# Packed constants, host-laid weights, joined u and v, and a planner with 24 rank settings in a one-layer encoder kernel

## The chip, the cores and the metric

The kernel runs on one core of a Trainium2 chip. The metric is the device time of one launch in microseconds (us). PE is TensorE with PEld its weight loads, DVE is VectorE, ACT is ScalarE, POOL is GpSimd, SP is SyncE, which issues most transfers.

## The reference

One layer of a bidirectional encoder on 1024 tokens of 1024 channels, all in float32:

```
h  = RMSNorm(x);  z = h @ w_in                      # 1024 x 3072, split into cv cg | lx lg | su sv
A  = silu(groupnorm(dwconv31(cv * sigmoid(cg))))    # 256 channels
B  = (rglru_fwd(lx) + rglru_bwd(lx)) * gelu(lg)     # 512 channels, gates from 8 heads of 64x64
C  = gelu(su) * (W_s layernorm(gelu(sv)) + b)       # 256 channels, chunks of 128 tokens
x  = x + concat(RMSNorm(A), RMSNorm(B), RMSNorm(C)) @ w_out
x  = x + (gelu(fg) * fu) @ w_down                   # fg, fu = halves of dwconv3(RMSNorm(x) @ w_up), 2 x 2816
x  = x + sigmoid(RMSNorm(x) @ w_ple_gate + b) * RMSNorm(p @ w_ple)
out = RMSNorm(x)
```

## The kernel before

Every float32 product is made of three matmuls of a rounded type (`mm3`): each operand is split into a high and a low part (`split`: ACT rounds the high part, DVE subtracts it), and high x high, high x low and low x high are summed in PSUM. A moving operand has 512 columns where it can.

The program is recorded first and ordered afterwards. Engine proxies (`Eng`, `Order.rec`) collect operations with costs; `rank` gives each a due time, counted back from the PE work in the order of recording, with three weights (`STRETCH`, how much slower than its cost a non-PE operation is taken to be; `FETCH`, how far ahead of its use a load is due; `DRAIN`, when a PSUM tile is to be emptied); `schedule` is a greedy list scheduler over the five queues (some ACT and DVE operations may change engine); `replay` runs the order through a model of waits and transfers, and its landing times go into the next of six rounds. The order with the shortest replay is issued. In the trace every instruction therefore has one line, L461, and is told apart by its tiles.

The stages, in the order of recording:

- Head. The eight tiles of x are loaded with SP (`load_x`, fixed first), normed, transposed by PE into hT, and multiplied into the first half of lx, two column tiles in matmuls of 256 columns.
- Constants. Fourteen small parameters are loaded by fifteen loads on POOL's queue (`rows`), as rows of 128 values, into tile V; `const_T` turns them into columns with five PE transposes, copies them out of PSUM with DVE (to cA, cB, cO in sm, cF) and makes what is derived from them: halves, sums, negatives, and log-sigmoid of lambda by a polynomial on 128x8 values.
- LRU (`lru(i)`, four blocks, two directions each): four taps over 1024 tokens, the first on ACT or DVE with scale and bias from cA, three on DVE; split; 12 matmuls against the gate weights; tanh, exp, sqrt; a scan on DVE. The gate weights of a block (`lru_gate_w`) are a memset of POOL and four POOL loads of 64x64 blocks into a 128x512 tile, then a split into V.
- Convolution (`conv_a`): 31 taps as 47 DVE operations of 512 columns per channel tile, from the gated product of cv and cg.
- p: its two halves are loaded token-major, transposed by PE (16 transposes), split, multiplied by w_ple and stored to DRAM (e).
- C: su and sv are two products with tokens on partitions (`token_major`), 256 columns each, sv first within each half of the tokens; `W0` to `W3` hold sv's weights, `W4`, `W5`, `G2`, `G3` those of su. The four spatial weight matrices are loaded as they are and transposed by PE. Then lg's products reuse W0 to W3.
- Join. C is scaled by a statistic that needs A's, transposed (`pt<-ident,xA`), and the first pass of w_out starts (`w_out_pass`).
- Up projection with a seven-product scheme on 256-column weight blocks (`prep_up`, `up_pair`, 20 of them, and two plain ones), the width-3 convolution and the gate on ACT and DVE; g goes through DRAM. Down projection, gate and final norm follow.

Weight blocks of 256 columns come through `load_cols`, in pieces of 256 values (1 KB):

```
S.dma_start(out=r[q], in_=w[q * 512:(q + 1) * 512, c0:c0 + 256].rearrange("(k p) c -> p k c", p=P))
```

Of the kernel before, what the change touches and what calls it, by code (L numbers as in the profile page):

```python
# [10 lines left out]
F32 = mybir.dt.float32  # L11
# [12 lines left out]
STRETCH = 2.2  # L24
DRAIN = 1.0
FETCH = 14.0
# [5 lines left out]
RATE = 330e3  # L32
ROUNDS = 6
# [25 lines left out]
class Vw:  # L59
# [18 lines left out]
    def flat(self):  # L78
        return Vw(self.tl, self.chain + [("rearrange", ("p a b -> p (a b)",))], self.idx.reshape(1, -1))
# [30 lines left out]
class Order:  # L110
# [125 lines left out]
    def rank(self):  # L236
# [6 lines left out]
        for op in self.ops:  # L243
            if op.eng != "P":
                for tl, m, w in op.acc:
                    if tl.psum and not w:
                        op.prio = min(op.prio, DRAIN + max(o.prio for o, _ in tl.wr if o.num < op.num))
        for op in reversed(self.ops):
            for d in op.deps:
                c = FETCH if d.calls[0][0] == "dma_start" else d.cost * (1 if d.eng == "P" else STRETCH)  # L250
                d.prio = min(d.prio, op.prio - c)
# [10 lines left out]
    def plan(self):  # L262
# [66 lines left out]
    def share(self, jobs):  # L329
        jobs.sort(key=lambda j: j[0])  # L330
        act, fin, t, i = {}, {}, 0.0, 0
        while i < len(jobs) or act:
            k = min(act, key=act.get) if act else None
            done = t + act[k] * len(act) / RATE if act else float("inf")
            step = min(done, jobs[i][0] if i < len(jobs) else float("inf"))
            for q in act:
                act[q] -= (step - t) * RATE / len(act)
            t = step
            if step == done:
                del act[k]  # L340
                fin[k] = t
            else:
                act[jobs[i][2]] = float(jobs[i][1])
                i += 1
# [128 lines left out]
def encoder_layer(ctx, tc, x, p, norm_mix, w_in, conv_dw_w, conv_dw_b, conv_gn_g, conv_gn_b,  # L473
                  lru_conv_w, lru_conv_b, lru_wa, lru_ba, lru_wx, lru_bx, lru_lambda,
                  sgu_ln_g, sgu_ln_b, sgu_ws, sgu_bs, out_norm, w_out, norm_ffn, w_up,
                  ffn_conv_w, ffn_conv_b, w_down, norm_ple, w_ple_gate, b_ple_gate, w_ple,
                  ple_post_norm, final_norm, out):
# [3 lines left out]
    x, p, out = x[0], p[0, 0], out[0]  # L481
    w_in, w_out, w_up, w_down = w_in[0], w_out[0], w_up[0], w_down[0]
# [57 lines left out]
    eps, cO = sm[:, 95:96], sm[:, 96:112]  # L540
# [7 lines left out]
    cA = blk("cA", [P, 108], F32)  # L548
    cB = blk("cB", [P, 110], F32)
    cS = blk("r16", [P, 32], F32)  # L550
    cF = blk("cF", [P, 176], F32)
    lg4, mv, st6 = cA[:, 76:92].cut(8), cA[:, 92:108].cut(2), cB[:, 62:110].cut(6)
    cB = cB[:, 0:62]

    load_table(AF.Sqrt, eps)

    def rows(dst, r0, n, src):
        G.dma_start(out=dst[r0:r0 + n, :], in_=src)
# [4 lines left out]
    def const_T():  # L563
        ps = pt()
        PE.transpose(ps[:, 0:74], stA[0:74, 0], ident[0:74, 0:74])
        PE.transpose(ps[:, 128:190], stA[0:62, 1], ident[0:62, 0:62])
        PE.transpose(ps[:, 256:272], stO[0:16], ident[0:16, 0:16])
        V.tensor_copy(cA[:, 0:74], ps[:, 0:74])
        V.tensor_scalar(out=cB, in0=ps[:, 128:190], scalar1=0.5, scalar2=None, op0=ALU.mult)
        V.tensor_copy(cO, ps[:, 256:272])  # L570
# [3 lines left out]
        ps = pt()  # L574
        PE.transpose(ps[:, 0:88], stF[0:88, 0], ident[0:88, 0:88])
        PE.transpose(ps[:, 128:216], stF[0:88, 1], ident[0:88, 0:88])
        V.tensor_copy(cF[:, 0:88], ps[:, 0:88])
        V.tensor_copy(cF[:, 88:176], ps[:, 128:216])
# [125 lines left out]
    st = blk("V", [P, 5, P])  # L704
    stA, stF, stO = st[:, 0:2], st[:, 2:4], st[:, 4]
# [10 lines left out]
    rows(stA[:, 0], O_CW, 32, lru_conv_w.rearrange("o d k (t p) -> (o d k t) p", p=P))  # L716
    rows(stA[:, 0], O_CB, 8, lru_conv_b.rearrange("o d (t p) -> (o d t) p", p=P))
    rows(stA[:, 0], O_BA, 8, lru_ba.rearrange("o d (t p) -> (o d t) p", p=P))
    rows(stA[:, 0], O_BX, 8, lru_bx.rearrange("o d (t p) -> (o d t) p", p=P))
    rows(stA[:, 0], O_LAM, 8, lru_lambda.rearrange("o d (t p) -> (o d t) p", p=P))  # L720
    rows(stA[:, 0], O_DB, 2, conv_dw_b.rearrange("o (t p) -> (o t) p", p=P))
    rows(stA[:, 0], O_SB, 4, sgu_bs.rearrange("o h p -> (o h) p"))
    rows(stA[:, 0], O_GN, 2, conv_gn_g.rearrange("o (t p) -> (o t) p", p=P))
    rows(stA[:, 0], O_GN + 2, 2, conv_gn_b.rearrange("o (t p) -> (o t) p", p=P))
    rows(stA[:, 1], 0, 62, conv_dw_w.rearrange("o k (t p) -> (o k t) p", p=P))
    rows(stO, 0, 8, out_norm.rearrange("o (k p) -> (o k) p", p=P))
    rows(stO, 8, 8, norm_ple.rearrange("o (k p) -> (o k) p", p=P))
# [12 lines left out]
    const_T()  # L740
# [133 lines left out]
    for h in range(2):  # L874
        pin = raw([P, 4, 256])
        S.dma_start(out=pin, in_=p.rearrange("(h t p) c -> h p t c", p=P, t=4)[h])
        for q in range(2):
            ps = pt()
# [17 lines left out]
    wsv = prep_cols(w_in, 1792, Mixed("W0", "W1", "W2", "W3"))  # L896
# [4 lines left out]
    S.dma_start(out=wsr, in_=sgu_ws[0].rearrange("h p q -> p h q"))  # L901
# [4 lines left out]
    wsu = prep_cols(w_in, 1536, Mixed("W4", "W5", "G2", "G3"))  # L906
# [488 lines left out]
```

## Time and profile before

| | |
|---|---|
| median of 3 runs | 1138.18 us (1138.13 to 1138.3) |
| profiled execution | 1138.66 us, span 1136.9 us |
| PE busy | 1109.4 us, 5305 matmuls |
| DVE busy | 820.5 us |
| ACT busy | 558.5 us |
| POOL busy | 25.5 us |
| HBM | 97 GB/s over the span |

The span runs from the first to the last instruction of the profiled execution. The ends of matmuls are modelled, so their starts give their pace.

### The profile page before, as it was taken

To read this page: it belongs to the slowest core of one execution; us is meant where nothing else is said; L and a number is where in the kernel's file an instruction comes from. 1 tells how busy PE (TensorE), PEld (TensorE's weight loads), DVE (VectorE), ACT (ScalarE), POOL (GpSimd) and SP (SyncE) were. 2 spreads that over 40 slices of the span, in tenths; PEclk is the share of its full clock that TensorE was granted. 3 is DMA by queue.
4 is the path that set the end of the run, shared out by engine and by line. 5 is a ranking of instruction groups with operands and counts; after the bars stand their busy time and mean duration, and the time that the engine had idled before them with its cause. 6 is when DMAs were issued, how large, how long until landed. Compare 5 with 4: busy or idle time off the path is not lost.

```text
span 1136.9 us, 13205 instructions
## 1 busy us (share of the span) xinstructions
PE 1109.4 (98%) x5305; PEld 929.8 (82%) x5305; DVE 820.5 (72%) x976; ACT 558.5 (49%) x720; POOL 25.5 (2%) x50
## 2 busy tenths in 40 slices
PE   6999999998999999999999999999999999999996
PEld 5987799887888888888888888888788888888885
DVE  6699999977966887687768776949433546654565
ACT  7555864779435475454545454536440222324445
POOL 3100100100000000000000000000000000000000
PEclk9999999999999999999999999999999999999999
DMA  8301240135032122232223222315640426421121
GB/s 296 99 1 56 94 162 20 53 101 185 22 122 96 39 74 93 75 111 74 69 80 112 74 74 75 111 56 192 235 147 2 148 85 212 130 75 40 72 74 55
DMA packets 55629, 110.60 MB, mean 97 GB/s; under 512 B 3977, under 2 KB 36594, under 8 KB 55568
## 3 DMA queue, kind: packets, MB, share of 16 engines
q1 hardware_dynamic: 53280, 104.35, 27.2%
q0 software_dynamic: 2288, 5.41, 1.3%
q8 instruction: 41, 0.67, 0.3%
q14 instruction: 20, 0.16, 0.0%
HBM read 85.63 MB, written 24.12 MB: 97 GB/s over the span
## 4 chain that ended last, share of the span: by engine, by line
PE 82%; DVE 13%; ACT 2%; issue 1%; DMA 1%; SPq 0%; DVEq 0%
PE pm L461 62%; PE pt L461 20%; DVE W L461 6%; DVE L L461 3%; DVE xA L461 1%; DMA xA<-in_x_dram 1%; DVE xB L461 1%; DVE G L461 1%; DVE hT L461 1%; ACT W L461 1%; ACT hT L461 0%; DMA raw<-in_w_down_dram 0%; ACT L L461 0%; ACT L461 0%; DVE V L461 0%
## 5 line engine op out<-in xcount | busy, mean ns | idle before, releaser
L461 PE MATMUL pm<-hT,W 128*128 128x512 f32 (+1 forms) x860 | 194.5, 369 | 0.1
L461 PEld LDWEIGHTS pm<-hT,W 128*128 128x128 f32 x860 | 149.8, 190 | 26.8 <-DVE hT L461 0.4
L461 PE MATMUL pm<-hT 128*128 128x512 f32 x480 | 124.6, 389 | 0.0
L461 PEld LDWEIGHTS pm<-hT 128*128 128x128 f32 x480 | 90.0, 188 | 19.2 <-DVE xA L461 0.4
L461 PE MATMUL pt<-hT,W 128*128 128x512 f32 x336 | 86.1, 389 | 0.0
L461 ACT ACTIVATE W<-raw 128x512 fp32r<-128x512 f32 (+1 forms) x60 | 44.9, 760 | 64.1 <-PE pt L461 47.8
L461 PEld LDWEIGHTS pt<-hT,W 128*128 128x128 f32 x336 | 63.1, 188 | 13.1
L461 DVE TENSOR_TENSOR xB<-xB,pm 128x512 f32<-128x512 f32 (+1 forms) x40 | 37.9, 950 | 42.5 <-PE pm L461 42.2
L461 PE MATMUL pm<-hT,hT 128*128 128x512 f32 (+1 forms) x256 | 66.2, 388 | 0.0
L461 ACT ACT_TABLE_LOAD x47 | 60.3, 1283 | 4.8 <-DVE W L461 2.4
L461 DVE TENSOR_TENSOR W<-raw,W 128x512 fp32r<-128x512 f32 (+1 forms) x57 | 47.1, 835 | 18.6 <-ACT W L461 18.6
L461 PEld LDWEIGHTS pm<-hT,hT 128*128 128x128 f32 x256 | 46.6, 188 | 8.9
L461 PE MATMUL pm<-L,L 128*128 128x512 f32 x160 | 50.3, 389 | 0.0
L461 DVE TENSOR_TENSOR xA<-xA,pm 128x1024 f32<-128x1024 f32 x20 | 24.4, 1219 | 35.1 <-PE pm L461 35.1
L461 DVE TENSOR_TENSOR X<-X,pm 128x512 f32<-128x512 f32 x20 | 13.7, 684 | 49.0 <-PE pm L461 49.0
L461 ACT ACTIVATE L<-raw 128x512 fp32r<-128x512 f32 (+1 forms) x19 | 15.8, 830 | 63.5 <-PE pm L461 35.0
L461 PE MATMUL pm<-xA,W 128*128 128x512 f32 x168 | 45.2, 389 | 0.0
L461 PE MATMUL pm<-W,hT 128*128 128x512 f32 x192 | 44.3, 390 | 0.0
L461 PE MATMUL pm<-L,hT 128*128 128x512 f32 (+1 forms) x160 | 43.7, 386 | 0.0
L461 ACT ACTIVATE hT<-raw 128x1024 fp32r<-128x1024 f32 x20 | 20.8, 1058 | 44.1 <-PE pm L461 31.4
L461 PEld LDWEIGHTS pm<-W,hT 128*128 128x128 f32 x192 | 35.9, 188 | 7.4
L461 PE MATMUL pt<-L,W 128*128 128x512 f32 x164 | 41.7, 390 | 0.0
(343 smaller groups left out, 2403.5 us busy)
## 6 DMA issues: line engine op xcount, KB each, us to landing
raw<-in_w_up_dram SPq DMA_DIRECT2D x44, 512.0 KB, 3.6
g<-xB SPq DMA_DIRECT2D x22, 512.0 KB, 2.7
raw<-g SPq DMA_DIRECT2D x22, 512.0 KB, 4.3
raw<-in_w_down_dram SPq DMA_DIRECT2D x22, 512.0 KB, 4.0
raw<-in_w_in_dram SPq DMA_DIRECT2D x16, 512.0 KB, 4.7
xA<-in_x_dram SPq DMA_DIRECT2D x8, 512.0 KB, 6.9
xB<-in_x_dram SPq DMA_DIRECT2D x8, 512.0 KB, 8.9
e<-L POOLq DMA_DIRECT2D x8, 512.0 KB, 3.2
```

The source lines that it names most:

```text
L461: getattr(self.e[op.eng], meth)(*args, **kw)
```

## The change

- The host concatenates the fourteen parameters and transposes them; one load on POOL's queue brings 128 x 328 values into the tile `cst`. `const_T` becomes `constants`, without its transposes and copies; the derived values stay.
- The host lays out each LRU block's gate weights as the 128x512 tile that the kernel wants, zeros included: one POOL load of 256 KB a block, no memset.
- The host gives p transposed (`p_t`) and the spatial weights transposed (`sgu_w`): both are loaded and split, without transposes.
- The first 1536 columns of w_in, and w_up, are stored as blocks of 256 columns, so that a partition's part of a load is 4 KB in one piece.
- su and sv are one product of 512 columns a token tile, with weights from `w_uv` in four loads, two k steps each.
- `plan` tries 24 settings of the three weights, three rounds each, and begins each setting without landing times from the one before. `share`, the replay's model of transfers, serves each queue in its order, at 310 in place of 330 GB/s.

```diff
-STRETCH = 2.2
-DRAIN = 1.0
-FETCH = 14.0
+RANKS = [(s, f, d) for s in (1.6, 1.9, 2.2, 2.5) for f in (9.0, 14.0) for d in (0.0, 1.0, 3.0) for _ in range(3)]
-RATE = 330e3
-ROUNDS = 6
+RATE = 310e3
...
-        for n in range(ROUNDS):
+        for n, (stretch, fetch, drain) in enumerate(RANKS):
+            if n % 3 == 0:
+                for op in self.ops:
+                    op.land = None
+            for op in self.ops:
+                op.eng, op.calls, op.cost = op.base
+            self.rank(stretch, fetch, drain)
             order = self.schedule()
             span = self.replay(order)
...
-    def const_T():
-        ps = pt()
-        PE.transpose(ps[:, 0:74], stA[0:74, 0], ident[0:74, 0:74])
...
-        V.tensor_copy(cA[:, 0:74], ps[:, 0:74])
-        V.tensor_scalar(out=cB, in0=ps[:, 128:190], scalar1=0.5, scalar2=None, op0=ALU.mult)
+    def constants():
+        V.tensor_scalar(out=cB, in0=cB, scalar1=0.5, scalar2=None, op0=ALU.mult)
...
-            S.dma_start(out=r[q], in_=w[q * 512:(q + 1) * 512, c0:c0 + 256].rearrange("(k p) c -> p k c", p=P))
+            S.dma_start(out=r[q], in_=w[c0 // 256, q].rearrange("p (k c) -> p k c", c=256))
...
-    rows(stA[:, 0], O_CW, 32, lru_conv_w.rearrange("o d k (t p) -> (o d k t) p", p=P))
...
+    G.dma_start(out=cst[:, 0:328], in_=consts)
...
         gwr = blk(tag, [P, 2, 2, P])
-        G.memset(gwr, 0.0)
-        for g, w in enumerate((lru_wa, lru_wx)):
-            for e in range(2):
-                G.dma_start(out=gwr[e * 64:(e + 1) * 64, :, g, e * 64:(e + 1) * 64],
-                            in_=w[0, :, 2 * i + e].rearrange("d p q -> p d q"))
+        G.dma_start(out=gwr.flat(), in_=lru_w[i])
...
-    for h in range(2):
-        pin = raw([P, 4, 256])
-        S.dma_start(out=pin, in_=p.rearrange("(h t p) c -> h p t c", p=P, t=4)[h])
-        for q in range(2):
-            ps = pt()
-            for j in range(4):
-                PE.transpose(ps[:, j * P:(j + 1) * P], pin[:, j, q * P:(q + 1) * P], ident)
-            split(pTh[q][:, h * 512:(h + 1) * 512], pTl[q][:, h * 512:(h + 1) * 512], ps)
+    for k in range(2):
+        a = raw([P, T])
+        S.dma_start(out=a, in_=p_t[k * P:(k + 1) * P, :])
+        split(pTh[k], pTl[k], a)
...
-    transposed(wsr.flat(), wsT[:, 0], wsT[:, 1])
+    split(wsT[:, 0], wsT[:, 1], wsr)
...
+    uring = Mixed("W0", "W1", "W2", "W3", "W4", "W5", "G2", "G3")
+    for q in range(4):
+        a = raw([P, 2, 512])
+        S.dma_start(out=a, in_=w_uv[q].rearrange("p (k c) -> p k c", c=512))
+        wuv.append((uring([P, 2, 512]), uring([P, 2, 512])))
+        split(*wuv[q], a)
...
+    def token_major(t):
+        ps, (hh, hl), c = pt(), hT[t // 4], slice((t % 4) * P, (t % 4 + 1) * P)
+        for k in range(KT):
+            w, j = wuv[k // 2], k % 2
+            mm3(ps, hh[:, k, c], hl[:, k, c], w[0][:, j], w[1][:, j], k == 0, k == KT - 1)
+        A.activation(out=gs[:, t], in_=ps, func=AF.Gelu_apprx_tanh)
```

## Rows read from the trace of the kernel before

**Rows 1.** The head of the page and its busy times

```profile
span 1136.9 us, 13205 instructions
...
PE 1109.4 (98%) x5305; PEld 929.8 (82%) x5305; DVE 820.5 (72%) x976; ACT 558.5 (49%) x720; POOL 25.5 (2%) x50
...
L461 ACT ACT_TABLE_LOAD x47 | 60.3, 1283 | 4.8 <-DVE W L461 2.4
```

**Rows 2.** Busy time by stretch: window and length, then busy us (instructions) of PE, PEld, DVE, ACT, POOL

```profile
0.00:25.00 25.00, 13.67 (x79) 12.46 (x80) 16.43 (x32) 16.98 (x31) 8.90 (x21) 1.00 0.93 314
25.00:50.00 25.00, 25.00 (x200) 24.32 (x197) 15.37 (x28) 13.51 (x22) 5.42 (x10) 1.00 0.35 114
...
75.00:207.00 132.00, 129.47 (x778) 114.36 (x777) 131.63 (x183) 87.79 (x106) 7.28 (x13) 1.00 0.22 75
207.00:255.00 48.00, 47.73 (x224) 39.62 (x224) 41.28 (x42) 34.73 (x39) 3.31 (x5) 1.00 0.23 76
255.00:275.00 20.00, 17.10 (x83) 13.76 (x82) 15.65 (x25) 19.39 (x21) 0.59 (x1) 0.91 0.59 186
275.00:375.00 100.00, 99.13 (x477) 82.39 (x476) 78.18 (x77) 47.04 (x80) 0.00 (x0) 1.00 0.26 92
375.00:800.00 425.00, 424.99 (x1874) 351.18 (x1873) 327.96 (x373) 217.94 (x273) 0.00 (x0) 1.00 0.26 88
```

**Rows 3.** The chain that ended last, from 73 to 207 us

```profile
by line: DVE W L461 48.8%; DVE L L461 21.1%; issue 7.9%; DVE xA L461 7.5%; DVE G L461 6.4%; DVE xB L461 4.6%; DVE cB L461 2.0%; DVE X L461 0.9%; DVE V L461 0.5%; DVE cA L461 0.4%; DVE r L461 0.2%; DVE sm L461 0.1%; DVEq L461 0.1%
```

**Rows 4.** POOL's timeline: start, us, operation, tiles, form [idle before <-releaser]

```profile
31.11 0.53 POOL L461 MEMSET L<- 128x512 f32 x1 [19.89 <-PE pt L461]
...
36.02 0.51 POOL L461 DMA_DIRECT2D V<-in_conv_gn_b_dram  x1
```

**Rows 5.** The timeline of all engines from 36 to 53 us

```profile
40.20 1.02 ACT L461 ACTIVATE X<-pm 128x1024 f32<-128x1024 f32 x1 [2.46 <-PE pm L461]
...
45.85 1.22 DVE L461 TENSOR_TENSOR W<-raw,W 128x1024 fp32r<-128x1024 f32 x1 [6.48 <-ACT W L461]
...
50.23 0.59 PE L461 MATMUL pt<-ident,V 74*128 74x74 f32 x3
...
50.75 1.64 PE L461 MATMUL pm<-hT,G 128*128 128x512 f32 x6
50.85 0.24 DVE L461 COPY cA<-pt 128x74 f32<-128x74 f32 x1 [1.30 <-PE pt L461]
...
51.13 0.17 DVE L461 TENSOR_SCALAR cA<-cA 128x16 f32<-128x16 f32 x1
...
51.44 1.23 ACT L461 ACTIVATE L<-X,cA 128x1024 f32<-128x1024 f32 x1
```

**Rows 6.** PE's timeline in three places: matmuls of 512 and 256 columns, transposes

```profile
63.10 8.32 PE L461 MATMUL pm<-hT,xA 128*128 128x512 f32 x36
71.27 1.52 PE L461 MATMUL pm<-hT,W 128*128 128x512 f32 x6
...
105.61 1.03 PE L461 MATMUL pt<-ident,raw 128*128 128x128 f32 x8
106.40 0.94 PE L461 MATMUL pm<-hT,W 128*128 128x512 f32 x3
...
166.24 1.60 PE L461 MATMUL pt<-G,hT 128*128 128x256 f32 x12
167.68 1.60 PE L461 MATMUL pt<-W,hT 128*128 128x256 f32 x12
```

**Rows 7.** PE's timeline around the join at 260 us

```profile
258.60 2.90 PE L461 MATMUL pm<-L,V 128*128 128x512 f32 x12
263.69 1.12 PE L461 MATMUL pt<-ident,xA 128*128 128x128 f32 x7 [2.18 <-DVE xA L461]
```

**Rows 8.** DMA issues: tiles, queue, count, size, median us to landing

```profile
raw<-in_w_up_dram SPq DMA_DIRECT2D x44, 512.0 KB, 3.6
...
raw<-in_w_down_dram SPq DMA_DIRECT2D x22, 512.0 KB, 4.0
```

More of the change, by code (lines that the diff above doesn't have):

```diff
@@ L78, in flat @@
     def flat(self):
-        return Vw(self.tl, self.chain + [("rearrange", ("p a b -> p (a b)",))], self.idx.reshape(1, -1))
+        names = " ".join("abc"[:self.idx.ndim - 1])
+        return Vw(self.tl, self.chain + [("rearrange", (f"p {names} -> p ({names})",))], self.idx.reshape(1, -1))
     def ap(self):
@@ L234, in link, with rank @@
                 d.users.append(op)
-    def rank(self):
+    def rank(self, stretch, fetch, drain):
         t = 0.0
@@ L246, in rank @@
                     if tl.psum and not w:
-                        op.prio = min(op.prio, DRAIN + max(o.prio for o, _ in tl.wr if o.num < op.num))
+                        op.prio = min(op.prio, drain + max(o.prio for o, _ in tl.wr if o.num < op.num))
         for op in reversed(self.ops):
             for d in op.deps:
-                c = FETCH if d.calls[0][0] == "dma_start" else d.cost * (1 if d.eng == "P" else STRETCH)
+                c = fetch if d.calls[0][0] == "dma_start" else d.cost * (1 if d.eng == "P" else stretch)
                 d.prio = min(d.prio, op.prio - c)
@@ L329, in share @@
     def share(self, jobs):
[L330 to L344, printed above, removed]
+        qs, fin, t = {}, {}, 0.0
+        for a, n, o in sorted(jobs, key=lambda j: j[0]):
+            qs.setdefault(o.base[0], []).append([a, float(n), o])
+        while any(qs.values()):
+            heads = [q[0] for q in qs.values() if q]
+            act = [h for h in heads if h[0] <= t + 1e-9]
+            if not act:
+                t = min(h[0] for h in heads)
+                continue
+            r = RATE / len(act)
+            step = min([h[1] / r for h in act] + [h[0] - t for h in heads if h[0] > t + 1e-9])
+            t += step
+            for h in act:
+                h[1] -= step * r
+                if h[1] <= 1e-6:
+                    fin[h[2]] = t
+                    qs[h[2].base[0]].pop(0)
         return fin
@@ L472, in encoder_layer @@
 @with_exitstack
[L473 to L477, printed above, removed]
+def encoder_layer(ctx, tc, x, p_t, norm_mix, w_in, w_uv, consts, lru_w, sgu_ln_g, sgu_ln_b, sgu_w,
+                  w_out, norm_ffn, w_up, w_down, w_ple_gate, b_ple_gate, w_ple, ple_post_norm,
+                  final_norm, out):
     nc = tc.nc
@@ L480, in encoder_layer @@
     V, A, PE, G, S = (Eng(od, e) for e in "VAPGS")
-    x, p, out = x[0], p[0, 0], out[0]
-    w_in, w_out, w_up, w_down = w_in[0], w_out[0], w_up[0], w_down[0]
+    x, out = x[0], out[0]
+    w_out, w_down = w_out[0], w_down[0]
     w_gate, w_ple = w_ple_gate[0], w_ple[0]
@@ L739, in encoder_layer @@
             mtile(wlx[0], c, hT, pss[c], [(n * P, 256)])
-    const_T()
+    constants()
     V.memset(centre, 0.0)
@@ L1364, in encoder_layer, with laid_out, blocks @@
         od.issue(order)
-_INS = ["x", "p", "norm_mix", "w_in", "conv_dw_w", "conv_dw_b", "conv_gn_g", "conv_gn_b",
-        "lru_conv_w", "lru_conv_b", "lru_wa", "lru_ba", "lru_wx", "lru_bx", "lru_lambda",
-        "sgu_ln_g", "sgu_ln_b", "sgu_ws", "sgu_bs", "out_norm", "w_out", "norm_ffn", "w_up",
-        "ffn_conv_w", "ffn_conv_b", "w_down", "norm_ple", "w_ple_gate", "b_ple_gate", "w_ple",
-        "ple_post_norm", "final_norm"]
-_OUTS = [((1, 1024, 1024), "float32")]
+_INS = ["x", "p_t", "norm_mix", "w_in", "w_uv", "consts", "lru_w", "sgu_ln_g", "sgu_ln_b", "sgu_w",
+        "w_out", "norm_ffn", "w_up", "w_down", "w_ple_gate", "b_ple_gate", "w_ple", "ple_post_norm",
+        "final_norm"]
+_OUTS = [((1, 1024, 1024), "float32")]
+def laid_out(i):
+    import numpy as _np
+    r = {n: i[n] for n in _INS if n in i}
+    r["p_t"] = i["p"][0, 0].T
+    w = i["w_in"][0]
+    def blocks(a, n):
+        m = 1024 // n
+        return a.reshape(8 // m, m, 128, -1, n).transpose(3, 0, 2, 1, 4).reshape(-1, 8 // m, 128, 1024)
+    r["w_in"] = blocks(w[:, :1536], 256)
+    r["w_uv"] = blocks(w[:, 1536:], 512)[0]
+    r["w_up"] = blocks(i["w_up"][0], 256)
+    names = ["lru_conv_w", "lru_conv_b", "lru_ba", "lru_bx", "lru_lambda", "conv_dw_b", "sgu_bs", "conv_gn_g",
+             "conv_gn_b", "conv_dw_w", "out_norm", "norm_ple", "ffn_conv_w", "ffn_conv_b"]
+    r["consts"] = _np.concatenate([i[n].reshape(-1, 128) for n in names]).T
+    g = _np.zeros((4, 2, 64, 2, 2, 2, 64), _np.float32)
+    for n, k in enumerate(("lru_wa", "lru_wx")):
+        v = i[k][0].reshape(2, 4, 2, 64, 64)
+        for e in range(2):
+            g[:, e, :, :, n, e] = v[:, :, e].transpose(1, 2, 0, 3)
+    r["lru_w"] = g.reshape(4, 128, 512)
+    r["sgu_w"] = i["sgu_ws"][0].transpose(2, 0, 1).reshape(128, 512)
+    return r
 def kernel(**inputs):
```

69 lines of the change are left out of this document (13 added, 56 removed).

## The prediction

> **What bounds the kernel now.** First the page's head and its table of engines [rows 1]: TensorE (PE) is busy 1109.4 of 1136.9 us, every other engine far less, so only two things can shorten the run: less matmul work, or fewer holes between matmuls. Then the stretches [rows 2], which the reader should scan for the PE column. From 375 to 800 us (the up projection) PE is busy 424.99 of 425 us: nothing done to loads or orders there can be worth anything. The holes lie early: 25.00 - 13.67 = 11.3 us in the first 25 us, then 132.00 - 129.47 = 2.5 us from 75 to 207, 0.3 us from 207 to 255, 2.9 us from 255 to 275 and 0.9 us from 275 to 375. From 75 to 207 the same rows show a second full engine: VectorE (DVE) is busy 131.63 of 132.00 us. The chain that ended last says which of the two decides there [rows 3]: from 73 to 207 us it runs through DVE almost alone (DVE W, the long tap sums of the conformer convolution, 48.8%; DVE L, the LRU, 21.1%). So between 73 and 207 DVE sets the pace and PE lives on filler; after that the chain is PE's again.
>
> Now look at where DVE's full stretch begins. POOL's queue holds the small constant loads; at 31.11 it had stood 19.89 us behind a MEMSET of a gate-weight block whose buffer was still being read, and the loads behind it went out only then, the last at 36.02 [rows 4]. They land as rows and need three PE transposes, which run at 50.23; DVE copies their result at 50.85, and the first tap of LRU 0 (ACT L<-X,cA) starts at 51.44, although its input X was evacuated from 40.20 to 41.22 [rows 5]. In these ten microseconds DVE does little: 6.48 us idle before 45.85, 1.30 us before 50.85 [rows 5], at least 7.8 us in all. The engine that is full for the next 132 us stands still because constants are late.
>
> **The change part by part.**
>
> *Constants.* Fifteen loads, five transposes and their four copies become one load of 128 x 328 values (168 KB) at the front of POOL's queue, ahead of every gate-weight load. PE: three transposes from 50.23 to 50.75 are 0.52 us [rows 5]; the other two add an estimated 0.1 us or more; I take 0.6 us. DVE: four copies of about 0.24 us, 1.0 us. The small arithmetic that stays (about 30 DVE instructions of 0.17 us [rows 5], 5 us) can move ahead of 41 us, where DVE is busy only 15.37 us in 25 [rows 2]. So DVE's full stretch can begin up to 10 us earlier and carry up to 5 us less. Not all of that can be had, since the convolution waits for PE's gate and value products: I take 10 us of lead; bounds 0 (the lead runs into that wait) and 15.
>
> *Cost of the same part.* The Exp of the lambda constants now may fall into the head, between the square roots of the first norm: two table loads of 1.28 us [rows 1] if it is put at a bad moment, 0 if it waits; I take 0. Gate weights come as four loads of 256 KB in place of sixteen of 32 KB and four MEMSETs; in the head that is 128 KB more for the first block, 0.4 us at the 314 GB/s of the first 25 us [rows 2]. If both POOL loads went ahead of the first tiles of x in full, (168 + 256) KB / 314 GB/s = 1.4 us. I take 0.4 us; range 0 to 1.4.
>
> *u and v joined.* Each token tile was 2 x 24 matmuls of 256 columns; it becomes 24 of 512. The trace has both paces: twelve of 256 start 1.44 us apart (166.24 to 167.68), 0.120 us each; thirty-six of 512 take 8.17 us (63.10 to 71.27), 0.227 us each [rows 6]. 384 x 0.120 = 46.1 us becomes 192 x 0.227 = 43.6 us: 2.5 us less PE work. ScalarE's evictions and DVE's statistics keep their element counts. Two waits come with it. First, the norm of the second half of v loses the cover of four u tiles (96 x 0.120 = 11.5 us); its mixed product comes some 5 us later, but what needs it, the transposes of C, run only at 263.69 [rows 7], and three more products of 48 x 0.227 = 10.9 us of the GeLU gate lie between: nothing. Second, W0 to W3 were free once v was done; now they are read until the last tile. The gate's weights are split into them, DVE's half 1.22 us [rows 5], ScalarE's half about as long. W0 and W1 hold the first two of eight k steps, so they come free 18 x 0.227 = 4.1 us before the tile ends, W2 and W3 2.7 us: covered, unless DVE is busy with something else, then up to 2.4 us of PE. I take 0.
>
> The Trainium skill (TensorE: Matmul & The Clock Gate, "Back-to-back issue gap") gives a warm matmul as N / 2.4 + 2.5 ns. By it the two paces would be 0.109 and 0.216 us, the products 41.9 and 41.4 us, and joining would be worth only 0.5 us. The trace disagrees with its 0.120 us per 256 columns [rows 6].
>
> *p and the spatial weights.* Sixteen transposes of p and four of the spatial weights go. Eight take from 105.61 to 106.40, 0.79 us [rows 6]: 20/8 x 0.79 = 2.0 us of PE. p is then split from a 1024-column load, two pairs in place of four half as long from PSUM; DVE saves a few tenths at most: 0.
>
> *w_in and w_up in blocks.* Each partition's 4 KB becomes contiguous in place of four 1 KB pieces. The page already shows what pieces of 1 KB cost: the w_up loads land in 3.6 us, the w_down loads, whose rows are 4 KB, in 4.0 us, both 512 KB [rows 8]; and PE has no hole in the up projection [rows 2]. 0, with bounds 0 and 0.5 us (two w_in loads stand ahead of the third x tile in the head).
>
> *The planner.* Before, six schedules of one set of weights; after, 24 sets of three, the best by its own replay, with a changed model of the DMA queues. It can only move holes. From 75 to 275 us there are 2.5 + 0.3 + 2.9 = 5.7 us of them. The 2.9 is one join: twelve LRU matmuls start at 258.60 and the transposes of C start at 263.69 after 2.18 us idle on DVE xA [rows 7]; a row of LRU passes had not come far enough. With constants 10 us earlier and PE done 5 us sooner, the join has 5 us more room than now. I take 4.5 of the 5.7 us, lead and planner together; bounds 0 and, with the 0.9 us up to 375, 6.6.
>
> **Sum.** PE work: 0.6 + 2.5 + 2.0 = 5.1 us. Holes: 4.5 us. Head: -0.4 us. Together 9.2 us. The profiled execution took 1138.66 us, its span 1136.9 us plus 1.8 us around it; its span would be 1127.7 us, its time 1129.5 us. It stood 0.5 us over the median of the timed runs, 1138.18 us, so I predict 1129 us.
>
> **Rivals.**
> *DVE stays the bound.* PE's 5.1 us come back as waiting, because the lead is lost in front of the convolution and only DVE's own 1.0 us of copies counts, less 0.4 us in the head: 1137.6 us; half and half gives 1134. For it: DVE full at 131.63 of 132.00 us [rows 2] and the chain [rows 3]. Against it: the idle DVE before 51 us [rows 5].
> *More than forecast.* The planner closes all 6.6 us up to 375 and a third of the head's 11.3 us, 3.8 us: 5.1 + 6.6 + 3.8 - 0.4 = 15.1 us, 1123 us. Against it: in the head x arrives at the rate of memory (DMA share 0.93 [rows 2]).
> *Slower.* The best replay may belong to a set that issues loads 9 us ahead of need in place of 14. The up projection has 20 block pairs, now without a hole [rows 2]. If each pair waited for its weights, PE would lose 20 times that wait; with 9.2 us gained elsewhere the kernel is slower by over 0.2% (2.3 us) from 0.58 us a pair on; at 0.7 us a pair it loses 14 us, gains 9.2 and ends near 1143 us. Against it: loads land in 3.6 us [rows 8], well within 9.
> *The skill's pace.* u and v bring 0.5 us, not 2.5: 1131 us, inside the forecast's range.
>
> **How the numbers follow.** Forecast 0.56 (1125 to 1133.5); the skill's pace 0.05; DVE stays the bound 0.22 (1133.5 to 1138.5, half of it within 0.2% of now); more than forecast 0.10; slower 0.07. 0.2%, 2.3 us, is about what a measurement of this kernel can tell from no change. Faster: 0.56 + 0.05 + 0.10 + 0.11 = 0.82; the same 0.11; slower 0.07. The range, 1122 to 1137.5, leaves out the slower case, a small part of the better one and the top of the DVE case.
>
> **What would show it.** After: no PE transposes of V or raw; the first LRU tap at about 42 us, not 51.44; DVE's full stretch starting ten microseconds earlier; 192 matmuls of 512 columns in the u|v stretch at 0.227 us; the join before the first output product with at most 1 us idle; 375 to 800 as full as now. I am wrong if the first tap still waits (for lambda's chain or the gate weights), if DVE idles in front of the convolution by what it gained, or if holes appear in the up projection.

## The result, and the profile after

The changed kernel takes 1149.72 us (median of 5 runs, 1145.24 to 1151.77) against 1138.18 us (1137.95 to 1139.7): ratio 1.0095, interval 1.0075 to 1.0116. It is slower by 11.5 us where 9.2 us of gain were forecast; the range 1122 to 1137.5 does not hold it. The profiled execution took 1149.67 us with a span of 1147.9 us.

The head of the page and its busy times, against [rows 1]:

```profile
span 1147.9 us, 12727 instructions
...
PE 1107.5 (96%) x5088; PEld 920.8 (80%) x5088; DVE 826.9 (72%) x970; ACT 552.1 (48%) x715; POOL 8.3 (1%) x20
...
L465 ACT ACT_TABLE_LOAD x44 | 56.5, 1283 | 6.8 <-DVE L L465 4.4
```

PE has 217 matmuls fewer: 192 of u and v, 25 transposes. So the work did go. The stretches, with the columns of [rows 2] (after the instruction counts: granted clock, DMA share, GB/s):

```profile
0.00:25.00 25.00, 7.14 (x35) 6.34 (x36) 16.22 (x52) 16.01 (x29) 1.91 (x8) 1.00 0.85 322
25.00:50.00 25.00, 25.00 (x215) 25.00 (x213) 21.07 (x41) 15.78 (x27) 0.54 (x1) 1.00 0.31 96
75.00:207.00 132.00, 125.60 (x552) 102.55 (x550) 127.61 (x167) 75.58 (x88) 4.80 (x9) 0.97 0.19 68
207.00:255.00 48.00, 47.12 (x227) 39.49 (x228) 35.65 (x48) 28.67 (x42) 0.55 (x1) 1.00 0.26 83
255.00:275.00 20.00, 18.55 (x92) 14.83 (x91) 18.08 (x27) 15.59 (x17) 0.00 (x0) 1.00 0.56 184
275.00:375.00 100.00, 97.46 (x437) 80.59 (x438) 70.70 (x69) 44.35 (x66) 0.53 (x1) 0.95 0.23 85
375.00:800.00 425.00, 424.08 (x1881) 350.75 (x1880) 337.00 (x373) 216.87 (x284) 0.00 (x0) 1.00 0.25 86
```

PE is less busy in the first 25 us (7.14 against 13.67), in 75 to 207 (125.60 against 129.47) and in 275 to 375 (97.46 against 99.13), and in the last two the granted clock is below 1. The up projection is as full as before but for two holes of about 0.6 us (at 377 and 426 us), which an operation of ACT and one of DVE end, not a load; so fetch and block layout are out of it.

A matmul that runs at half clock counts as busy too, so I also count **holes**: the time from one matmul's start to the next, less the pace of its width (0.227, 0.120 or 0.108 us for 512, 256 and 128 columns), summed. Before: first matmul at 7.97 us, holes 23.1 us, last matmul's end at 1127.60. After: 14.64, 32.7 and 1138.63. What is left is matmul work: 1096.5 and 1091.3 us. So work -5.2, later start +6.7, holes +9.6: +11.1 us, against the 11.0 us between the profiled times. A hole is not all waiting: at half clock matmuls of 512 columns start 0.427 us apart (150.06 to 151.34, three of them, below), and the 0.2 us beyond the pace count as hole. By that an estimated 7.2 us of the holes after, and 1.6 of those before, are slow matmuls, so some 5.6 of the 9.6 us are the clock's.

*The head.* All engines around the first norm, in order of time:

```profile
7.91 0.21 ACT L465 ACTIVATE L<-cst 128x8 f32<-128x8 f32 x1 [5.59 <-DMA cst<-in_consts_dram]
7.92 0.17 DVE L465 TENSOR_SCALAR cst<-cst 128x16 f32<-128x16 f32 x1 [6.08 <-DMA cst<-in_consts_dram]
...
8.14 1.28 ACT L465 ACT_TABLE_LOAD   x1
...
9.43 0.21 ACT L465 ACTIVATE L<-L 128x8 f32<-128x8 f32 x1
9.55 1.04 ACT L465 ACTIVATE L<-xA 128x1024 f32<-128x1024 f32 x1
...
10.70 1.28 ACT L465 ACT_TABLE_LOAD   x1
...
11.62 0.42 DVE L465 CAST V<-L 128x512 fp32r<-128x512 f32 x1
...
13.21 1.28 DVE L465 SCALAR_TENSOR_TENSOR L<-xA,sm,X 128x1024 f32<-128x1024 f32 x1
...
14.64 0.45 PE L465 MATMUL pt<-ident,L 128*128 128x128 f32 x1 [14.64 <-DVE L L465]
```

ACT stands 5.59 us for the constants (Abs of lambda), loads the Exp table, and only then takes the first square of x (9.55; 4.45 in the kernel before), then loads the Sqrt table again. Not all of the 5.59 us is lost, since x itself had to land: from 4.45 on, ACT loses 3.5 us waiting, 1.6 to Abs, Exp and its table, and then 1.3 to the Sqrt table. That is 6.4 of the 6.7 us by which PE starts later; the gate-weight split on DVE (from 11.62) stands ahead of the norm's last steps and adds a little. The kernel before had its first square, and its first constant load, so:

```profile
1.46 0.65 POOL L461 DMA_DIRECT2D V<-in_lru_conv_w_dram  x1 [0.16 <-issue]
...
4.45 1.06 ACT L461 ACTIVATE L<-xA 128x1024 f32<-128x1024 f32 x1 [2.12 <-DMA xA<-in_x_dram]
```

```profile
V<-in_lru_conv_w_dram POOLq DMA_DIRECT2D x1, 16.0 KB, 5.7
```

After the change, the DMA view, beside [rows 8], says why (median us to landing at the end); POOL's timeline, against [rows 4], has the load out at 1.44:

```profile
raw<-in_w_up_dram SPq DMA_DIRECT2D x44, 512.0 KB, 3.4
...
L<-in_lru_w_dram POOLq DMA_DIRECT2D x4, 256.0 KB, 3.3
...
cst<-in_consts_dram POOLq DMA_DIRECT2D x1, 164.0 KB, 6.5
```

```profile
1.44 0.68 POOL L465 DMA_DIRECT2D cst<-in_consts_dram  x1
2.12 0.54 POOL L465 DMA_DIRECT2D L<-in_lru_w_dram  x1
```

*125 to 175 us, holes 9.5 us (before 1.7).* PE and ACT around the end of the p product:

```profile
148.61 1.65 PE L465 MATMUL pm<-W,xA 128*128 128x512 f32 x3 [3.03 <-ACT pm L465]
150.06 1.48 PE L465 MATMUL pm<-G,xA 128*128 128x512 f32 x3
151.34 1.48 PE L465 MATMUL pm<-W,xA 128*128 128x512 f32 x3
...
158.82 1.06 ACT L465 ACTIVATE W<-raw 128x1024 fp32r<-128x1024 f32 x1
159.78 1.04 ACT L465 ACTIVATE G<-raw 128x1024 fp32r<-128x1024 f32 x1
...
162.81 0.98 PE L465 MATMUL pm<-L,V 128*128 128x512 f32 x3 [1.57 <-ACT pm L465]
163.63 4.28 PE L465 MATMUL pt<-W,hT 128*128 128x512 f32 x18
```

PE waits for ACT's eviction and square of a p tile (3.03 us), the clock is halved from 146.9 to 153.8 us (three matmuls then start 1.45 us apart, 148.61 to 150.06, in place of 0.68), and u|v starts only after its last weights are split into tiles that held the p product's weights to its end. The row at 162.81 does not show PE waiting for those weights, though: it waits 1.57 us for ACT's square of the last p tile, and on ACT the two splits (158.82 and 159.78) had gone ahead of that tile.

The joined tiles themselves run as forecast, 24 matmuls of 512 columns in 5.44 us (0.227 each):

```profile
169.11 5.60 PE L465 MATMUL pt<-W,hT 128*128 128x512 f32 x24
174.55 0.84 PE L465 MATMUL pt<-G,hT 128*128 128x512 f32 x3
```

*255 to 275 us.* The join, against [rows 7], waits 1.32 us where it waited 2.18; the holes of 250 to 275 us fell from 5.3 to 2.7:

```profile
270.40 1.23 PE L465 MATMUL pt<-ident,xA 128*128 128x128 f32 x8 [1.32 <-DVE xA L465]
```

*300 to 350 us, holes 7.7 us (before 1.0).* PE where the two output passes meet:

```profile
314.14 0.39 PE L465 MATMUL pm<-L,hT 128*128 128x512 f32 x1
315.90 0.50 PE L465 MATMUL pm<-L,hT 128*128 128x512 f32 x1 [1.37 <-DVE L L465]
...
318.23 0.79 PE L465 MATMUL pm<-L,G 128*128 128x512 f32 x1 [0.64 <-DVE G L465]
...
320.10 3.41 PE L465 MATMUL pt<-ones,L 128*128 128x2 f32 x16
...
324.80 5.49 PE L465 MATMUL pm<-W,hT 128*128 128x512 f32 x17
```

The second pass's first tile stands ahead of the rest of the first pass and waits for DVE's splits; 24 matmuls that need nothing (W,hT from 324.80; the view ends at 330 us and shows 17) are queued behind it. The clock is halved from 317.6 to 327.8 us, and an estimated 4.6 of the 7.7 us are matmuls at that clock, the rest the waits.

*DVE's lead.* The forecast's first tap came at 45.50 us (before 51.44 [rows 5]); then:

```profile
67.61 0.69 DVE L465 TENSOR_TENSOR V<-L,V 128x512 fp32r<-128x512 f32 x1 [4.11 <-ACT V L465]
...
73.85 1.23 DVE L465 SCALAR_TENSOR_TENSOR L<-L,L 128x1024 f32<-128x1024 f32 x1 [1.93 <-ACT L L465]
```

DVE idles 7.3 us between 50 and 75 (3.4 before), all of it in front of operations of the LRU that wait for ACT. The first scan starts at 76.4 (91.6), but the convolution's first tap at 92.4 (73.0) and the last scan at 302.1 (296.6). The convolution came later because the plan had put the LRU ahead of it, on PE too: the last matmuls of its value product (pm<-hT,xA) start at 88.51, and in the kernel before they were through when the next began at 71.27 [rows 6].

```profile
88.51 1.52 PE L465 MATMUL pm<-hT,xA 128*128 128x512 f32 x6
```

### The profile page after: what moved, and what is told of

Read it like the earlier page. It is cut to its first block, busy times and chain, and to the rows that moved or that the text cites. A ratio compares the mean times of both kernels' runs of the same rounds, so it can differ in the third digit from the quotient of the medians.

```text
span 1147.9 us, 12727 instructions
## 1 busy us (share of the span) xinstructions
PE 1107.5 (96%) x5088; PEld 920.8 (80%) x5088; DVE 826.9 (72%) x970; ACT 552.1 (48%) x715; POOL 8.3 (1%) x20
## 4 chain that ended last, share of the span: by engine, by line
PE 76%; DVE 8%; issue 1%; ACT 1%; DMA 1%; DVEq 0%; SPq 0%
PE pm L465 56%; PE pt L465 20%; DVE L L465 3%; DVE W L465 2%; DVE G L465 1%; DVE xA L465 1%; DMA xA<-in_x_dram 1%; DVE X L465 1%; DVE hT L465 0%; ACT W L465 0%; DVE xB L465 0%; DVE cst L465 0%; ACT pm L465 0%; DVE r L465 0%; ACT L465 0%
## 5 line engine op out<-in xcount | busy, mean ns | idle before, releaser
L465 PE MATMUL pm<-hT,W 128*128 128x512 f32 (+1 forms) x860 | 188.0, 368 | 1.0 <-ACT L L465 1.0
L465 DVE SCALAR_TENSOR_TENSOR W<-xB,cst,W 128x513 f32<-128x513 f32 (+1 forms) x88 | 60.8, 739 | 0.0
L465 ACT ACTIVATE W<-L 128x1024 fp32r<-128x1024 f32 x14 | 14.8, 1061 | 68.4 <-PE pm L465 68.4
```

Source lines behind the costliest of these rows:

```text
L465: getattr(self.e[op.eng], meth)(*args, **kw)
```

## The experiments

One table first; the medians of the kernel before lay between 1137.87 and 1138.34 us beside them. "First" is the first matmul's start; the four columns of holes are us from that start to 25, 125 to 175, 175 to 275 and 300 to 350; "half" is the time at half clock before the last matmul. These columns come from the one profiled execution of each kernel, which lay within 1.7 us of the median, but for e10 (1151.59, 3.2 below it).

| kernel | median us | ratio (interval) | first | to 25 | 125-175 | 175-275 | 300-350 | half |
|---|---|---|---|---|---|---|---|---|
| before | 1138.18 | 1 | 7.97 | 8.0 | 1.7 | 7.9 | 1.0 | 3.4 |
| the change | 1149.72 | 1.0095 (1.0075 to 1.0116) | 14.64 | 6.5 | 9.5 | 5.2 | 7.7 | 17.1 |
| e1 | 1149.91 | 1.0096 (1.0081 to 1.0111) | 12.01 | 7.4 | 8.7 | 4.3 | 4.1 | 10.2 |
| e2 | 1146.46 | 1.0071 (1.0053 to 1.0088) | 15.43 | 7.0 | 6.2 | 8.1 | 1.8 | 0 |
| e3 | 1137.88 | 0.9999 (0.9989 to 1.0008) | 7.93 | 7.7 | 2.6 | 5.2 | 3.7 | 0 |
| e4 | 1146.22 | 1.0067 (1.0052 to 1.0082) | 14.44 | 6.4 | 8.1 | 6.6 | 4.0 | 6.8 |
| e5 | 1138.07 | 0.9999 (0.9989 to 1.0008) | 7.91 | 7.9 | 7.4 | 6.3 | 1.0 | 10.2 |
| e6 | 1141.80 | 1.0027 (1.0016 to 1.0039) | 14.91 | 7.0 | 5.0 | 4.6 | 1.8 | 3.4 |
| e7 | 1136.46 | 0.9985 (0.9974 to 0.9996) | 14.76 | 6.7 | 5.9 | 3.4 | 0.8 | 6.8 |
| e8 | 1136.17 | 0.9984 (0.9975 to 0.9994) | 8.08 | 7.8 | 5.9 | 3.7 | 0.3 | 3.4 |
| e9 | 1131.20 | 0.9938 (0.9923 to 0.9953) | 8.05 | 8.1 | 3.4 | 4.1 | 1.2 | 0 |
| e10 | 1154.77 | 1.0144 (1.0126 to 1.0163) | 14.73 | 6.9 | 9.6 | 4.8 | 8.7 | 13.7 |
| e11 | 1141.32 | 1.0029 (1.0018 to 1.0041) | 8.11 | 12.0 | 6.8 | 3.3 | 1.0 | 0 |
| e12 | 1131.91 | 0.9950 (0.9933 to 0.9967) | 8.05 | 8.4 | 3.4 | 4.1 | 1.4 | 0 |
| e13 | 1134.46 | 0.9968 (0.9957 to 0.9979) | 7.88 | 7.4 | 2.4 | 4.2 | 3.4 | 0 |
| e14 | 1142.79 | 1.0049 (1.0029 to 1.0068) | 14.60 | 6.6 | 9.5 | 5.3 | 1.0 | 6.8 |
| e16 | 1139.21 | 1.0007 (0.9998 to 1.0016) | 7.97 | 7.7 | 0.8 | 4.9 | 4.9 | 3.4 |
| e17 | 1134.23 | 0.9964 (0.9952 to 0.9975) | 8.05 | 8.3 | 3.2 | 4.0 | 1.9 | 0 |

**Planner or data? (e2, e3, e4).** e2 is the change with the planner of before; e3 is the kernel before with the planner of the change; e4 is the change with one set of rank weights, (2.2, 9, 0).

```diff
 e4
-RANKS = [(s, f, d) for s in (1.6, 1.9, 2.2, 2.5) for f in (9.0, 14.0) for d in (0.0, 1.0, 3.0) for _ in range(3)]
+RANKS = [(s, f, d) for s in (1.6, 1.9, 2.2, 2.5) for f in (9.0, 14.0) for d in (0.0, 1.0, 3.0) for _ in range(3)][36:39]
```

> The changed kernel's data and arithmetic with the planner of before: one set of weights, six rounds, the old model of transfers. Theory A and its sister (the plan that was picked has holes that the replay did not see): 1140 to 1145 us, since some 5 us less matmul work stands against a head that may still be late. Rival C: the new layouts themselves (joined u and v, one product with all eight weight tiles held to its end) make the middle slower whatever the plan: 1147 us or more.

> The kernel of before with the planner of after: constants still land as rows and pass through PE, so the head can't be late through them. If the search over 24 sets is worth something on the chip: 1130 to 1135 us. If the replay's choice means nothing there (theory: its best order is no better than any other): 1137 to 1146 us.

> The changed kernel with one set of weights in place of 24: stretch 2.2, fetch 9, drain 0, the second best by the replay, about a microsecond behind the set that was picked. If the picked order was unlucky in its holes after 140 us (three waits there, two of them followed by a halved clock): 1142 to 1146 us. If the loss lies in the head, which this order shares: 1148 to 1151 us.

The planner by itself brings nothing (e3, 0.9999; 1137.88 us, where a gain would have been 1130 to 1135), and with either planner the new data lose 8.1 to 11.5 us. e2 (1146.46) fell between its two theories and e4 (1146.22) just outside the first of its two, so neither decides alone. Three orders of the same data lie 3.5 us apart (1146.2 to 1149.7): differences of that size between two planned kernels carry no weight alone.

**The head (e1, e5, e11).** e1 keeps the change's order, and moves the constants' operations as one block behind the last operation of the eighth norm. e5 plans anew with one more dependence:

```diff
 e5, in link():
+            if op.num > self.normed.num and any(d.eng == "G" for d in op.deps):
+                op.deps.add(self.normed)
```

> The changed kernel's order, with the arithmetic on the constants (Abs, Exp of lambda and some 30 small DVE operations) held behind the norm of the eighth x tile; nothing else moves. Theory A: the head is late because ACT and DVE stand in order behind the constants' load and two table loads, and nothing later makes up for it. Then the first transposes start at about 8 us, not 14.6, the lx products end about 5 us sooner, and the time is 1144 to 1145.5 us. Rival B: what counts lies after 60 us (DVE-bound stretch, order of the plan), and a head that is 5 us shorter is waited out before 320 us. Then 1148 to 1150 us.

> The change, with one new dependence for the planner: no instruction that reads a load of POOL's queue (constants, LRU gate weights) may stand ahead of the eighth norm's last vector operation; everything else is planned as in the change. Theory 'head': the late start of TensorE (first matmul at 14.64 us against 7.97) comes from ACT, DVE and the table loads being spent on constants that land at 7.9 to 9.4 us; freed of them TensorE starts at 8 to 9.5 us and the run takes 1143 to 1145 us (1149.7 less 5 to 6). Rival 'given back': the constants' 26 small vector operations then stand in front of the first taps as in the kernel before, and the gain is lost at the waits of 125 to 175 us: TensorE starts at 8 to 9.5 us and the run still takes 1148 to 1150 us.

e1 (1149.91 us) did not do what theory A needed: the gate weights of the LRU stayed ahead of the norm, and the block put in one piece only moved the wait: start and first holes together fell from 21.1 to 19.4 us, and a new hole stands at 40.55. Its time lies where rival B has it, but as the head was hardly freed it says little on B. Its VectorE, then its TensorE:

```profile
9.31 0.43 DVE L465 CAST V<-L 128x512 fp32r<-128x512 f32 x1 [7.47 <-DMA L<-in_lru_w_dram]
```

```profile
40.55 0.88 PE L465 MATMUL pt<-ident,L 128*128 128x128 f32 x4 [4.61 <-DVE hT L465]
```

e5 has both readers behind the norms. PE starts at 7.91 and the run takes 1138.07 us, 11.7 us less than the change, where 5 to 6 were expected: start and first holes together give 5.3 us (21.1 to 15.8), the rest is mainly the hole of 300 to 350 us (7.7 to 1.0). The loads themselves did no harm: in e5 both are issued as before (1.44 and 2.11 us) and land as late (6.2 and 7.3 us after issue), yet the first square of x starts at 4.34. Where the later hole is gone already, the same rule gives what the head alone costs: 5.3 us with e7's tiles (e7 to e9) and 5.6 with u and v split (e6 to e8), against rival B and "given back".

e11 has no rule; it gives the planner two numbers of the trace (four more lines use them):

```diff
+def lag(op, t):
+    return 1.1 if op.eng == "S" else 4.8 if t < 6 else 2.0
...
-        free = {e: 0.0 for e in self.e}
+        free = {e: 1.44 if e == "G" else 0.0 for e in self.e}
```

> The change with its planner told two numbers that the trace of the change shows: POOL issues its first load at 1.44 us, not at 0, and a load that POOL issues in the first 6 us lands some 4.8 us later than its bytes alone would take. No rule on what may go ahead of what. Theory 'head': the planner put the constants' work in front of the norms because it thought them landed by then; told the truth it puts them behind by itself, TensorE starts at 8 to 9.5 us and the run takes 1137 to 1140 us, as the kernel with the rule (1138.07). Rival: the planner still puts part of them ahead (start 10 to 13 us) and the run takes 1143 to 1148 us.

1141.32 us lies between the two theories. The first tile went first (8.11), but the constants, Exp and its table, and two splits of weights came ahead of the copies that empty the first tile's transposes out of PSUM; the second tile's waited for them, and start and holes together are 20.1 us:

```profile
16.21 1.97 PE L469 MATMUL pt<-ident,L 128*128 128x128 f32 x8 [6.16 <-DVE hT L469]
```

A truer landing time alone was not enough here; e5's rule was.

**Sharing tiles with the p product (e6, e7, e9, e12, e16, e17).** e6 splits u and v again. e7 gives the p product's weights other tiles:

```diff
 e7
-    wple_r = Mixed("W4", "W5", "G2", "G3")
+    wple_r = Mixed("Y0", "S0", "W6", "G3")
```

> The change, but u and v are again two products of 256 columns with weights in eight-tile halves (v in W0 to W3, u in W4, W5, G2, G3), as in the kernel before; all other parts of the change stay. Theory 'shared tiles': the joined product can't start before the p product has released W4, W5, G2 and G3, and this makes the holes of 150 to 175 us (3.7 us in the change); split again they shrink to about 1 us while the work of TensorE grows by 2.5 us: 1148 to 1150 us, no gain. Rival 'the joining is the main loss': the holes at 125 to 175 us (9.5 us) all go, and the run takes 1142 to 1144 us. Rival 'joining has nothing to do with it': holes as in the change and 2.5 us more work, 1152 us.

> The change, but the weights of the p product stand in other tiles (three that are free then, and G3), so that the joined u|v weights share one tile of eight with them instead of four. Theory 'shared tiles': the splits of the u|v weights no longer wait for the p product's end, the hole at 161 us (1.7 us) and part of the 3.2 us at 145 us go: 1145 to 1147.5 us. Rival 'ScalarE's evictions': the p product is held by ScalarE (an eviction and an in-place square of 1024 columns for every tile), the weights come late for the same reason, and the run stays at 1149 to 1150 us.

e6 came out at 1141.80, near what the rival "the joining is the main loss" said, though with holes in the middle left (5.0 us): PE's longest wait there, for ACT in the p product, is as long with u and v split (3.15 us at 151.94). e7 took 1136.46, 13.3 us less than the change, where its theory had 2 to 5; only 3.6 us of it lie in 125 to 175, where ACT's evictions still hold PE:

```profile
156.25 2.56 PE L465 MATMUL pm<-centre,xB 128*128 128x128 f32 x16 [2.33 <-ACT pm L465]
```

Again the hole of 300 to 350 us is gone in both, so neither tells its own cost by itself.

e9 is e5 and e7 together, e12 the same with the planner of before, e17 is e9 with u and v split, e16 the control: the kernel before with the new planner and e7's line.

> Both of the two edits before together: no reader of POOL's loads ahead of the eighth norm, and the p product's weights in tiles of their own but one. If the two causes are separate and add up: TensorE starts at 8 to 9.5 us, no hole over 1 us at 150 to 175 us, 1139 to 1142 us. If a saving in the head is only given back at the next wait: 1146 to 1149 us. The sum that the blind forecast went by (5 us less work of TensorE, no new waits) would give 1133 to 1134 us.

> The kernel with both edits (no reader of POOL's loads ahead of the eighth norm; the p product's weights in tiles of their own but one), planned by the planner of the kernel before: one set of rank weights, its six rounds, its model of the queues. Theory 'data': what the two edits brought (1131.2 us) lies in the data's layout and the buffers, and the old planner gets it to within 2 us: 1129.5 to 1133.5 us. Rival 'luck of an order': the old planner's order of the same kernel loses at other waits: 1136 us or more.

> The kernel before with the new planner, and only the p product's weights in tiles of their own but one. Control for the kernel with both edits (1131.2 us). If that kernel is fast because of the change's own savings, once their waits are gone, this one stays at 1137 to 1139 us (u's weights share those tiles too, but they are wanted only behind v, 11.5 us later). If moving these tiles is a gain by itself, unrelated to the change, it comes to 1135 us or less.

> The kernel with both edits (1131.2 us), but u and v as two products of 256 columns again. What joining is worth when its weights have tiles of their own: by the paces of the trace (0.120 us per 256 columns, 0.227 per 512) 2.5 us, so 1133 to 1134.5 us. If the cover of v by u is worth as much as the columns, 1130.5 to 1132 us.

e9 takes 1131.20 us (1131.0 to 1131.37): faster than both kernels, 18.5 us below the change, 6.7 below before (1137.87 beside it), and faster than any of the three theories had it. Its stretches:

```profile
0.00:25.00 25.00, 13.13 (x77) 11.80 (x78) 16.03 (x33) 16.68 (x31) 1.91 (x8) 1.00 0.81 311
...
75.00:207.00 132.00, 129.54 (x593) 106.56 (x592) 129.23 (x178) 82.94 (x101) 4.83 (x9) 1.00 0.21 74
...
275.00:375.00 100.00, 99.06 (x475) 82.36 (x474) 80.19 (x80) 45.04 (x78) 0.00 (x0) 1.00 0.21 74
```

PE is as busy as in [rows 2] at full clock throughout. It is not the luck of one order: the old planner gets 1131.91, as the theory "data" said. In the kernel before, moving the tiles is no gain: e16 takes 1139.21. With the change's data it is, and most with u and v joined: 6.9 us joined (e5 to e9) against 1.9 split (e8, below, to e17), which two orders can differ by. Read the other way, joining is worth 3.0 us with the tiles free (1134.23 to 1131.20, forecast 2.5) and costs 1.9 with them shared (1136.17 to 1138.07). The 3.0 has the count of matmuls behind it; the 1.9, which would turn the sign, is again no more than the spread of orders, and the 5.0 us between the two is not much beyond it.

How sharing tiles costs the time is not shown. No wait for a shared tile is among PE's long ones. In e5 the longest of 125 to 175 is 4.15 us for ACT's square of a p tile (at 147.52), and ACT had stood 4.90 us in front of an LRU tap that waited for DVE; in e9, with other tiles and so another order, that wait is gone.

**Both costs away, joining undone (e8).** e5's rule and e6's split.

> The change with no reader of POOL's loads ahead of the eighth norm, and with u and v as two products of 256 columns again (the p product's weights stay where they were). So what is left of the change is packed constants, p and spatial weights laid out by the host, the blocks and the new planner, without its two costs. If the head's 5.3 us (start) and what goes with it add to the 7.9 us that splitting u and v brought: 1133 to 1136 us. If both edits cure the same late wait (the hole of 300 to 325 us is gone in either alone): 1136 to 1138 us.

1136.17: e5 and e6 alone bring 11.7 and 7.9 us, together 13.6. They overlap by 6.0 us, about the hole of 300 to 350 us that goes in either (6.7 and 5.9 us), as the second theory said.

**The hole at 314 us (e10, e14).** The change's own order, only the second pass's first tile moved behind the first pass:

```diff
     order = od.plan()
+    first = next(i for i, o in enumerate(order) if od.psB in o.dyn or o in od.std)
+    last = order.index(od.lastA)
+    held = []
+    for o in order[first:last]:
+        if od.psB in o.dyn or o in od.std or o.deps & set(held):
+            held.append(o)
...
+    rest = [o for o in order[first:last + 1] if o not in held]
+    order[first:last + 1] = rest + held
```

e10 has this without `od.std`, the sixteen matmuls with a column of ones.

> The change's own order of instructions, with one thing moved: the matmuls of the second output pass's first token tile (and what depends on them) stand behind the last tile of the first pass, not in front of its last third. In the change TensorE waits there for VectorE's splits (1.37, 0.23 and 0.64 us at 315.9 to 318.2), its clock is at half for 10.2 us from then on, and its holes of 300 to 350 us sum to 7.7 us, while 17 matmuls that need nothing (3.9 us) stand behind. Theory 'order': these fill the hole, and the run takes 1143 to 1146 us (4 to 6 us less than 1149.7). Rival 'VectorE is late': the first pass ends earlier, the same splits are waited for just behind it, and only 0 to 2 us are won: 1148 to 1150 us.

> The change's own order again, with the second output pass's first tile and the sixteen matmuls with a column of ones (the norm's sum over tokens) both put behind the last tile of the first pass. In the run before, the ones' matmuls had stayed in front and took over the whole wait (5.33 us for VectorE's L, then 24 matmuls of the first pass, 5.4 us, still to do). Theory 'order': the 24 matmuls fill the wait, VectorE's L is there at 318.9 us just as they end, TensorE's clock stays full, and the run takes 1142 to 1145 us. Rival 'VectorE is late for the whole second pass': the wait comes back at its first tiles and 1148 us or more is measured.

e10 was worse, 1154.77: the ones' matmuls stood next in line and took the whole wait over. PE of e10, then of e14:

```profile
318.94 3.57 PE L465 MATMUL pt<-ones,L 128*128 128x2 f32 x16 [5.33 <-DVE L L465]
322.37 7.11 PE L465 MATMUL pm<-W,hT 128*128 128x512 f32 x24
```

```profile
313.60 5.74 PE L465 MATMUL pm<-W,hT 128*128 128x512 f32 x24 [0.51 <-DVE xB L465]
319.18 0.62 PE L465 MATMUL pm<-hT,hT 128*128 128x512 f32 x2
...
322.58 1.84 PE L465 MATMUL pt<-ones,L 128*128 128x2 f32 x16
```

In e14 the 24 matmuls fill the wait, the clock stays full there, and the run takes 1142.79 us, 6.9 less, as the theory "order" said; in its row of the table only the hole and the half clock there moved. e7 and e9 also put second-pass matmuls ahead of the first pass's last 24 (W,hT at 310.36 and 302.80) and lose nothing; their last scans start at 291.1 and 289.5 us, the change's at 302.1. So the order cost only where DVE was late. Why DVE was late in the change, and not in e5 to e9, was not traced.

**Constants by themselves (e13).** e7 with the old constants and gate-weight loads, transposes and memsets.

> The change without its packed constants: constants and LRU gate weights are loaded in many pieces and transposed as in the kernel before; p, the spatial weights, u|v, the blocks and the new planner as in the change, and the p product's weights in tiles of their own but one. The forecast priced the constants' part at 0.6 us of TensorE and a lead of 10 us for VectorE that was to close 4.5 us of holes. Theory 'the lead is worth what was forecast': against the kernel with packed constants out of the head (1131.2 us) it loses 4 to 5 us: 1135 to 1136.5 us. Rival 'the lead runs into later waits': it loses only the 0.6 us of transposes, 1131 to 1132.5 us. Should it be faster than 1130.5 us, packing the constants costs time by itself.

1134.46 us (1132.87 to 1136.7), between the theories: packing them out of the head (e9) is worth 3.3 us, 0.6 of it transposes; the rest is within what two orders can differ by.

**What the loss is made of.** From e9 to the change, 18.5 us, each cost was also taken out by itself: the head 5.3 us (e7 to e9), the shared tiles 6.9 (e5 to e9), the hole at 314 us 6.9 (e14, where the order is the change's own). They sum to 19.1.

## Why the prediction was wrong

- *PE work, -5.1 us:* right. Measured 5.2 us, at the pace that was forecast.
- *Head, "I take 0.4 us; range 0 to 1.4" and the table loads "0 if it waits; I take 0":* the first step that failed. Two table loads of 1.28 us did fall between the norms, but they are the smaller part: ACT stood for the load behind which it was put, 3.5 us beyond the moment when x had let the kernel before begin. I had priced the bytes, not the landing, and the bytes cost nothing that e5 shows. The row was in the trace of before: POOL's first small constant load, 16 KB, took 5.7 us to land; at that, one issued at 1.44 lands at 7.1 us, 2.7 us after the first square of x began. The head cost 5.1 us (16.0 to 21.1), and e5 gives it back (5.3 and 5.6 us in the other two pairs). The Trainium skill (DMA: Bandwidth & Descriptors, "Anatomy of one DMA — SWDGE (gpsimd) path") puts a transfer from GpSimd at 2.0 us plus its bytes over 436 GB/s, an estimated 2.4 us for this load; the trace does not agree, with 6.5 us among the head's transfers. The Trainium skill (ScalarE: Activation LUTs, "Table sets: the hidden batching unit") says to do all of one table set before the next; the trace agrees that breaking this brought two loads, but at 1.28 us each (the Exp behind the first starts 1.29 us after it, 8.14 to 9.43), not the about 2.7 us that it puts beside one load.
- *u and v joined, waits "I take 0":* the second. The forecast looked at W0 to W3 and the gate's weights; the other four, W4, W5, G2 and G3, are held by the p product, and u's weights used to be wanted 11.5 us later, under the cover of v. The cover was priced for the statistics and not for the buffers. e5 to e9 put the sharing at 6.9 us with joining; without it, e16 shows none and e8 to e17 1.9. That the term was not 0 is shown; that the cost is a wait for these tiles is not, since PE's long waits there are for ACT, and how much comes from the order planned around the sharing was not separated.
- *Holes, -4.5 us, bounded by 0 and 6.6:* the third. Holes grew by 9.6 us, and a planned order was taken to be unable to lose. 6.7 of them are one place (e14): a tile put ahead by the plan, with DVE late. The clock, which the sum had no term for, is part of it: half clock before the last matmul went from 3.4 to 17.1 us. This hole is not what lost the range by itself: without it the time is still outside (e14, 1142.79). The planner as such: 0 (e3). The join's stretch lacked 2.9 us of PE before and 1.5 after (18.55 of 20); counted as holes of 250 to 275, 2.6 us were won, and more was spent elsewhere.
- *DVE's lead, 10 us:* the mechanism held only for the first tap (5.9 us earlier). The lead was lost much as the forecast's own sign of being wrong had it: DVE idled 7.3 us before the convolution began, though for ACT's part of the LRU, and its last scan came 5.5 us later than before.
- *Rivals:* "slower" had the side and not the mechanism; the up projection kept up (424.08 of 425 us). "DVE stays the bound" had the lost lead, but its price stops at no gain. With the head's rule and other tiles (e9) the kernel takes 1131.2 us, near the forecast's 1129; but that is another kernel, and no credit to the forecast. ("Half and half gives 1134" is 1133.3 by the rival's own numbers; nothing hangs on it.)

## What to carry to other kernels

An early load is free only for engines that are not made to wait for it: read the landing time of that queue's loads in that stretch of the trace, and look what stands behind the first reader on the same engine, which takes its instructions in order. When two products become one, list all buffers that the new one needs at its start and who holds them until when; the cover that vanishes may have covered them too. And a list of holes that a better order might close is also a list of places where a late engine can open more, so the bound of such a term has both signs.

## What was not expected of the hardware

At half clock the sixteen matmuls with two columns take 3.41 us, and 1.84 us at full clock (e14). The clock fell after some holes and not after others of the same length: in e6 a hole of 3.3 us at 148 us was followed by 3.4 us at half clock, in e11 one of 3.3 us at 153 us by none. What decides it was not tried. With such a stretch a hole costs more than its wait: at 314 us the waits were about 3.2 us and the slow matmuls after them an estimated 4.6.

POOL's loads of 4 KB in the head of the kernel before took 5.3 to 6.1 us to land, nearly as long as the one of 164 KB after they were packed (6.5 us); the four gate-weight loads of 256 KB land in 3.3 us in the median, the one in the head in 7.2.
